# Opening of the prompt attention: constant loads on GpSimd's queue, cache copies behind the fourth store, bias turned after two projections

## The chip, the cores and the metric

The kernel runs on one NeuronCore of a Trainium2 chip. Each engine works through its own list of instructions strictly in order: TensorE (PE, with its weight loads as PEld), VectorE (DVE), ScalarE (ACT), GpSimd (POOL) and SyncE (SP). SP computes nothing; it issues the DMA transfers, and POOL can issue transfers too, on a queue of its own, between its arithmetic. The metric is device time in microseconds (us) for one execution. Two kernels are called different from about 0.2% on.

## The reference

One inference step of a decoder layer, for a prompt of 2048 tokens and 8 single-token samples, width 1024:

```python
q_a, k_a, v_a, q_g, k_g, v_g, r_g, log_a = project(rmsnorm(xp, attn_norm_g), w_in, ...)
o_a = prompt_window_attention(q_a, k_a, v_a, rel_bias, attn_sinks)   # 128-row blocks, own and previous keys
o_g, s_p = gla_chunked(q_g, k_g, v_g, log_a, s0)                     # gated linear attention
xp = finish(xp, o_a, o_g, r_g, ...)                                  # W_o, residual, SwiGLU feed-forward
# the same for the 8 samples, with cached keys and values; their window is shifted by one position:
k_win_sample = concat(cache_k, k_new)[:, -128:]
v_win_sample = concat(cache_v, v_new)[:, -128:]
```

The softmax attention adds a bias that depends only on the distance of query and key (a table `rel_bias` of 32 buckets by 8 heads) and has one learned sink per head. Queries and keys are normalised per head, with gains `q_norm_g` and `k_norm_g`.

## The kernel before, in words

The program has three stages: A, the projections for the softmax attention and the attention itself, in 16 blocks of 128 tokens; B, the gated linear attention; C, the output projection and the feed-forward part by one level of Strassen products. Every float32 product is made of three matmuls on a high and a low part (`mm3`, L107 to L109): high by high, high by low, low by high. `split` (L95 on ACT, L96 on DVE) makes the two parts, so each weight that comes in is cast by ACT and subtracted by DVE before PE may use it.

The part at stake is the first 60 us of stage A. `front(b)` (L290 on) loads a block `xt` of the input, squares and sums it on ACT (L134), forms the variance on DVE (L114, `rs_v`), takes the power -1/2 on POOL (L115, `rs_r`), scales the block on DVE (L137), transposes it in eight matmuls on PE (L142, tile `ps_nT`) and splits it into `nT`. The first block's tile is `xt_181` in the lists below. `load_wq`, `load_wkv`, `load_lr` fill `WA`, the 784 columns of the weights for queries, keys, values and the gate's low rank; `load_wr` fills `WR`, 512 columns. `project(b)` multiplies a block with `WA` (24 matmuls of 512 columns and 24 of 272), `project_r(b)` with `WR` (24 of 512), `attend(b)` does the attention and ends with a store of its output to `mix_d` in DRAM (L422). `load_gains` (L209) loads the gains and sinks, `make_bias` (L521) builds the bias: it loads `rb`, `oh`, `aq`, `afterK` and `flip`, multiplies `rb` with `oh` (L536, `ps_ext`), stores the 8 x 256 result in DRAM (`ext_d`), reads it back with overlapping rows (`rev`, L546) and turns it with the matrix `flip` on PE (L548, `ps_rev`). `decode_a` is the samples' attention, advanced a piece per block.

What sets the order: the code is written once, and when the program is built a scheduler lays out each engine's list by its own estimate of when each instruction's inputs will be there. So a line that moves in the code, or goes to another queue, can shift instructions of other lines. A second rule concerns transfers: SP's issues use eight counters in turn (`DMAHW0` to `DMAHW7` in the lists, `DMASW0` to `DMASW7` for POOL's), and an issue that comes round to a counter waits until the transfer that used it before has landed.

Of the kernel before, what the change touches and what calls it, by code (L numbers as in the profile page):

```python
# [20 lines left out]
P = 128  # L21
# [5 lines left out]
HD = 64  # L27
# [19 lines left out]
def bcast_rows(ap_1d, n, parts=P):  # L47
    return bass.AP(ap_1d.tensor, ap_1d.offset, [[0, parts], [1, n]])
# [3 lines left out]
def hymba_kernel(ctx: ExitStack, tc: tile.TileContext, I, O, X=None, phases=3):  # L52
    nc = tc.nc
# [12 lines left out]
    mix_d = [dram.tile([P, KD, P], F32, name=f"mix_d{i}") for i in range(NB)]  # L66
# [27 lines left out]
    def split(h, l, src, eng=None):  # L94
        nc.scalar.copy(h, src)  # L95
        (eng or nc.vector).tensor_tensor(l, src, h.bitcast(F32), ALU.subtract)  # L96
# [50 lines left out]
    with ExitStack() as ph:  # L147
# [58 lines left out]
        gkB = pc.tile([P, HD], F32, name="gkB")  # L206
        sinkB = pc.tile([P, 8], F32, name="sinkB")

        def load_gains():  # L209
            for g, nm in ((gq, "q_norm_g"), (gk, "k_norm_g")):  # L210
                for h in range(2):
                    nc.sync.dma_start(g[h * 64:(h + 1) * 64], I[nm].rearrange("o d -> d o"))
            nc.vector.tensor_scalar(gq, gq, 0.125, None, ALU.mult)
            nc.sync.dma_start(sinkB, bcast_rows(I["attn_sinks"], 8))
            nc.sync.dma_start(gkB, bcast_rows(I["k_norm_g"], HD))

# [3 lines left out]
        afterK = pc.tile([P, P], F32, name="afterK")  # L222
# [11 lines left out]
        def dense(nT, n, W, c0, c1):  # L234
            ps = acc.tile([P, 512], F32, tag="acc", name="ps_d")
            for k in range(KD):
                mm3(ps[:n, :c1 - c0], nT[:, 0, k, :n], nT[:, 1, k, :n], W[:, 0, k, c0:c1], W[:, 1, k, c0:c1],
                    k == 0, k == KD - 1)
            return ps
# [11 lines left out]
        def gate_r(ps, n):  # L251

            r = rp.tile([P, 512], F32, tag="r", name="r", bufs=2)
            t = rp.tile([P, 512], F32, tag="rt", name="rt", bufs=1)
            nc.scalar.copy(r[:n], ps[:n])
            nc.gpsimd.tensor_scalar(t[:n], r[:n], -87.0, None, ALU.max)
            nc.scalar.activation(t[:n], t[:n], AF.Exp, scale=-1.0)
            nc.scalar.activation(t[:n], t[:n], AF.Ln, bias=1.0)
            nc.scalar.activation(t[:n], t[:n], AF.Exp, scale=-1.0)
            nc.gpsimd.tensor_tensor(r[:n], r[:n], t[:n], ALU.mult)  # L260
            return r
# [92 lines left out]
        def project_r(b):  # L354
            pr = dense(nTs.pop(b), P, WR, 0, 512)
            r = gate_r(pr, P)
            nc.sync.dma_start(r_d[b], r)

        def attend(b):
# [4 lines left out]
            nm = small.tile([P, 8], F32, tag="nm", name="nm")  # L364
# [3 lines left out]
            for v in range(2):  # L368
                St = sp.tile([P, 4, P], F32, tag="S", name="S")
                S.append(St)  # L370
                for c2 in range(2):
                    ps = scp.tile([P, 512], F32, tag="sc", name="ps_s")
                    for c in (2 * c2, 2 * c2 + 1):
                        o = (c % 2) * 256
# [7 lines left out]
                    for c in (2 * c2, 2 * c2 + 1):  # L382
                        o = (c % 2) * 256
                        h = 4 * v + c
# [5 lines left out]
                for c in range(4):  # L390
                    h = 4 * v + c
# [6 lines left out]
            o = wl.tile([P, 512], F32, tag="o", name="o", bufs=2)  # L398
            ol = wl.tile([P, 512], F32, tag="ol", name="ol", bufs=1)
            lo, hi = slice(0, 64), slice(64, 128)  # L400
            for v, (rh, rl) in enumerate(((lo, hi), (hi, lo))):
# [17 lines left out]
                        nc.tensor.matmul(po, dv[:, v], pa[:, i], start=False, stop=i == 1)  # L419
                nc.scalar.copy(ol[rh], po[rl])  # L420
                nc.vector.tensor_tensor(o[rh], po[rh], ol[rh], ALU.add)
            nc.sync.dma_start(mix_d[b][:, 0:4, :], o.rearrange("p (c t) -> p c t", c=4))  # L422

        def decode_a():
            with ExitStack() as decs:
# [95 lines left out]
        def make_bias():  # L521


            with tc.tile_pool(name="a_ext", bufs=1) as ep:
                rb = ep.tile([N_BUCKETS, 8], F32, name="rb")
                nc.sync.dma_start(rb, I["rel_bias"])
                oh = ep.tile([N_BUCKETS, 256], F32, name="oh")
                nc.sync.dma_start(oh, I["c_onehot"])
                aq = ep.tile([P, P], F32, name="aq")
                nc.sync.dma_start(aq, I["c_after"][0])  # L530
                nc.vector.tensor_copy(afterQ, aq)
                nc.sync.dma_start(afterK, I["c_after"][1])
                flip = ep.tile([P, P], F32, name="flip")
                nc.sync.dma_start(flip, I["c_flip"])
                ps = aux.tile([P, 512], F32, tag="aux", name="ps_ext")
                nc.tensor.matmul(ps[:8, :256], rb, oh, start=True, stop=True)  # L536
                ext = rp.tile([P, 512], F32, tag="rt", name="ext", bufs=1)[:8, :256]
                nc.scalar.copy(ext, ps[:8, :256])
                nc.sync.dma_start(ext_d, ext)

                nc.sync.dma_start(dbias_d[:, 1:P], ext[:, 0:P - 1])
                nc.sync.dma_start(dbias_d[:, 0:1], ext[:, P - 1:P])

                for g in range(2):
                    rev = ep.tile([P, 4, P], F32, tag="rev", name="rev", bufs=2)
                    nc.sync.dma_start(rev, bass.AP(ext_d.tensor, ext_d.offset + g * 1024, [[1, P], [256, 4], [1, P]]))  # L546
                    ps = ppp.tile([P, 512], F32, tag="pp", name="ps_rev")
                    nc.tensor.matmul(ps, flip, rev.rearrange("p h j -> p (h j)"), start=True, stop=True)  # L548
                    nc.vector.tensor_copy(bias[:, 4 * g:4 * g + 4].rearrange("p h j -> p (h j)"), ps)
# [8 lines left out]
        load_wkv(0)  # L558
        load_wkv(4)
        load_gains()  # L560
        make_bias()
        for k in range(0, KD, 2):
            load_wr(k)
        project(0)
        project(1)
        project_r(0)
        project_r(1)
        dec = decode_a()
        for b in range(NB):
            if b + 2 < NB:  # L570
                front(b + 2)
            if 1 < b + 1 < NB:
                project(b + 1)
                if b + 1 < NB - 2:
                    project_r(b + 1)
            attend(b)
            if b >= 1:
                next(dec, None)
            if b == 3:
                nc.sync.dma_start(gg, I["gla_norm_g"].rearrange("o d -> d o"))  # L580
                w2 = pc.tile([16, 256], F32, name="w2")
                nc.sync.dma_start(w2, I["w_gla_gate2"][0])
                split(w3[0:16], w3[64:80], w2)
                nc.vector.tensor_copy(w3[32:48], w3[0:16].bitcast(F32))
                for p in range(2):
                    nc.sync.dma_start(bT[:, p:p + 1], I["b_gla_gate"][0:1, p * P:(p + 1) * P].rearrange("o d -> d o"))
                nc.gpsimd.tensor_scalar(nbT, bT, -1.0, None, ALU.mult)
                for nm_, cache in (("k_win_sample", "cache_k"), ("v_win_sample", "cache_v")):
                    nc.sync.dma_start(O[nm_][0, :, 0:P - 1].rearrange("n t h d -> n t (h d)"),
                                      I[cache][0, :, 1:P].rearrange("n t h d -> n t (h d)"))  # L590
        project_r(NB - 2)
        project_r(NB - 1)
    if phases < 2:
# [890 lines left out]
```

## Time and profile before

| | us |
|---|---|
| median of 3 runs (2256.2 to 2256.39) | 2256.27 |
| the profiled execution | 2255.43 |
| its span, first to last instruction | 2253.3 |
| PE busy in it | 2186.8 (97%) |
| DVE, ACT, POOL busy | 1584.1, 981.7, 687.1 |
| clock granted to TensorE, mean | 0.991 |

The profiled execution is 0.84 us below the median, and 2.1 us of it lie outside the span. The views used below are: the list of who waited for whom; the timeline of one engine (start, duration, what, and in brackets the idle time before it with what ended it); tables of busy time by stretches of the span, with the granted clock and the DMA engines' share; groups of instructions by line; and the list of transfers with their sizes. A matmul's duration in the timeline overlaps that of the next one, so the cost of one in a row of them is read from the distance of two starts.

### The profile page before, as it was taken

Reading aid. Unit: us, or ns where it says so; the run is one execution under the profiler, and the core shown is the slowest. Engines: PE = TensorE matmul, PEld = TensorE weight load, DVE = VectorE, ACT = ScalarE, POOL = GpSimd, SP = SyncE. Lnnn points to the kernel's source line nnn. Section 1 sums busy time; section 2 is a strip of 40 time slices with the busy share of each in tenths; the row PEclk is TensorE's granted clock in tenths of the full one; section 3 lists DMA queues with packets and bytes.
Section 4 is the critical chain, followed back from the end, with each engine's and each line's share of the span. In section 5 each row is a group of like instructions: output and inputs, shape, how many; then the busy total and the mean of one; then the engine's idle time right before and its main releaser. Section 6 shows DMA issues by size and latency. Waiting matters only on the chain.

```text
span 2253.3 us, 34780 instructions
## 1 busy us (share of the span) xinstructions
PE 2186.8 (97%) x12573; PEld 1886.2 (84%) x12573; DVE 1584.1 (70%) x3129; ACT 981.7 (44%) x2249; POOL 687.1 (30%) x781
## 2 busy tenths in 40 slices
PE   7999998999998999999999999999999899999997
PEld 5788887888886888688888889999999878787886
DVE  6788888777865666766666666676766765757487
ACT  5656666465654334333333333333333344434342
POOL 2555665564653223211111120111111122222222
PEclk9999999999999999999999999999999999999999
DMA  7323325444507998942333385333333477879786
GB/s 226 110 76 119 118 77 188 133 156 157 184 24 268 318 326 263 327 127 81 112 97 111 95 284 183 90 104 89 113 97 92 152 189 178 195 169 234 165 210 232
DMA packets 212331, 364.32 MB, mean 162 GB/s; under 512 B 15768, under 2 KB 129456, under 8 KB 209072
## 3 DMA queue, kind: packets, MB, share of 16 engines
q1 hardware_dynamic: 175104, 258.63, 35.2%
q0 software_dynamic: 37056, 103.47, 18.1%
q8 instruction: 99, 1.62, 0.3%
q14 instruction: 72, 0.59, 0.1%
HBM read 210.83 MB, written 152.29 MB: 161 GB/s over the span
## 4 chain that ended last, share of the span: by engine, by line
PE 74%; DVE 10%; issue 6%; DMA 5%; ACT 4%; POOL 2%; SPq 0%; POOLq 0%; DVEq 0%; ACTq 0%
PE ps_b L108 7%; PE ps_b L107 7%; PE ps_b L109 7%; PE ps_c L108 5%; PE ps_c L107 5%; PE ps_c L109 5%; PE ps_a L108 5%; PE ps_a L107 5%; PE ps_a L109 5%; PE ps_wo L107 3%; PE ps_wo L108 3%; PE ps_wo L109 3%; DMA z<-zc_d_P 1%; PE ps_l L850 1%; PE ps_v L107 1%
## 5 line engine op out<-in xcount | busy, mean ns | idle before, releaser
L107 PE MATMUL ps_b<-z,whl 128*128 128x258 f32 (+1 forms) x792 | 254.1, 321 | 1.2 <-ACT whl L95 1.2
L109 PE MATMUL ps_b<-z,whl 128*128 128x258 f32 (+1 forms) x792 | 253.0, 319 | 1.6 <-DVE whl L96 1.6
L108 PE MATMUL ps_b<-z,whl 128*128 128x258 f32 (+1 forms) x792 | 254.3, 321 | 0.0
L95 ACT CAST dm<-mr 128x384 fp32r<-128x384 f32 (+1 forms) x224 | 108.5, 488 | 188.3 <-PE ps_b L109 105.2
L108 PE MATMUL ps_a<-z,whl 128*128 128x258 f32 (+1 forms) x528 | 169.2, 320 | 0.0
L108 PE MATMUL ps_c<-z,whl 128*128 128x258 f32 (+1 forms) x528 | 169.1, 320 | 0.0
L109 PE MATMUL ps_a<-z,whl 128*128 128x258 f32 (+1 forms) x528 | 168.9, 320 | 0.0
L107 PE MATMUL ps_c<-z,whl 128*128 128x258 f32 (+1 forms) x528 | 168.7, 319 | 0.3 <-DMA z<-zc_d_P 0.3
L109 PE MATMUL ps_c<-z,whl 128*128 128x258 f32 (+1 forms) x528 | 168.9, 320 | 0.0
L107 PE MATMUL ps_a<-z,whl 128*128 128x258 f32 (+1 forms) x528 | 168.8, 320 | 0.0
L109 PEld LDWEIGHTS ps_b<-z,whl 128*128 128x128 f32 x792 | 149.4, 189 | 14.4 <-DVE whl L96 2.3
L107 PEld LDWEIGHTS ps_b<-z,whl 128*128 128x128 f32 x792 | 149.5, 189 | 13.1 <-ACT whl L95 1.3
L108 PEld LDWEIGHTS ps_b<-z,whl 128*128 128x128 f32 x792 | 149.4, 189 | 11.9
L96 DVE TENSOR_TENSOR dm<-mr,dm 128x384 fp32r<-128x384 f32 (+1 forms) x224 | 115.1, 518 | 57.4 <-ACT dm L95 57.3
L95 ACT CAST whl<-wrg 128x512 fp32r<-128x512 f32 x132 | 81.5, 619 | 154.8 <-PE ps_b L109 81.3
L1316 POOL DMA_DIRECT2D md_d<-m x22 | 15.7, 712 | 360.7 <-DVE m L1279 360.7
L1017 DVE TENSOR_TENSOR gu<-ps_c,gu 128x512 f32<-128x512 f32 (+1 forms) x130 | 77.9, 599 | 59.5 <-PE ps_c L109 58.8
L96 DVE TENSOR_TENSOR whl<-wrg,whl 128x512 fp32r<-128x512 f32 x132 | 90.7, 688 | 37.9 <-ACT whl L95 37.5
L845 POOL TENSOR_TENSOR bd<-E,qTb 64x256 f32<-64x256 f32 x112 | 102.2, 913 | 41.4 <-ACT E L833 26.5
L95 ACT CAST whl<-sy 128x512 fp32r<-128x512 f32 x88 | 54.6, 620 | 132.1 <-PE ps_b L109 84.7
L107 PEld LDWEIGHTS ps_c<-z,whl 128*128 128x128 f32 x528 | 99.8, 189 | 8.6 <-issue 0.7
L107 PEld LDWEIGHTS ps_a<-z,whl 128*128 128x128 f32 x528 | 99.7, 189 | 8.0
(404 smaller groups left out, 6683.6 us busy)
## 6 DMA issues: line engine op xcount, KB each, us to landing
mr<-md_d SPq DMA_DIRECT2D x24, 1344.0 KB
zc_d_P<-zhl POOLq DMA_DIRECT2D x56, 512.0 KB, 6.5
z<-zc_d_P SPq DMA_DIRECT2D x14, 2048.0 KB
wrg<-in_w_gate_dram SPq DMA_DIRECT2D x44, 512.0 KB
wrg<-in_w_up_dram SPq DMA_DIRECT2D x44, 512.0 KB
nT_d<-nT SPq DMA_DIRECT2D x16, 1024.0 KB
zT<-nT_d SPq DMA_DIRECT2D x8, 2048.0 KB
h_d<-gu POOLq DMA_DIRECT2D x48, 256.0 KB, 4.7
```

The source lines that it names most:

```text
L95: nc.scalar.copy(h, src)
L96: (eng or nc.vector).tensor_tensor(l, src, h.bitcast(F32), ALU.subtract)
L107: nc.tensor.matmul(ps, lh, rh, start=start, stop=False, skip_group_check=more)
L108: nc.tensor.matmul(ps, lh, rl, start=False, stop=False, skip_group_check=more)
L109: nc.tensor.matmul(ps, ll, rh, start=False, stop=stop, skip_group_check=more)
L845: nc.gpsimd.tensor_tensor(bv[rows, h], E5[rows, :, :, 1], qv[rows, :, :, 1], ALU.mult)
L850: nc.tensor.matmul(ps[:, g * P:(g + 1) * P], Ef[:, g * P:(g + 1) * P], bd[:, :, g], start=True, stop=True)
L1017: nc.vector.tensor_tensor(out, a, b, ALU.add)
L1316: nc.gpsimd.dma_start(md_d[sb][g][:, :, q, fp - GROUPS[g][0], :], src.rearrange("p (m t) -> p m t", m=4))
```

## The change

Three edits, none of which changes what is computed:

- the eleven small loads of `load_gains` and of `make_bias` (gains, sinks, the bias table, masks, the flip matrix; the largest have 64 KB) are issued by POOL in place of SP;
- `make_bias` becomes a generator with one stop: up to the stores of the 8 x 256 table it runs where it stood, its second part (`rev`, the turning matmul, the copy to `bias`) comes in the code after `project(0)` and `project(1)`;
- the two DRAM-to-DRAM copies of the cached keys and values into the samples' windows (508 KB each) may be issued only after the store of the fourth block's attention output.

```diff
         def load_gains():
             for g, nm in ((gq, "q_norm_g"), (gk, "k_norm_g")):
                 for h in range(2):
-                    nc.sync.dma_start(g[h * 64:(h + 1) * 64], I[nm].rearrange("o d -> d o"))
+                    nc.gpsimd.dma_start(g[h * 64:(h + 1) * 64], I[nm].rearrange("o d -> d o"))
             nc.vector.tensor_scalar(gq, gq, 0.125, None, ALU.mult)
-            nc.sync.dma_start(sinkB, bcast_rows(I["attn_sinks"], 8))
-            nc.sync.dma_start(gkB, bcast_rows(I["k_norm_g"], HD))
+            nc.gpsimd.dma_start(sinkB, bcast_rows(I["attn_sinks"], 8))
+            nc.gpsimd.dma_start(gkB, bcast_rows(I["k_norm_g"], HD))
...
-            nc.sync.dma_start(mix_d[b][:, 0:4, :], o.rearrange("p (c t) -> p c t", c=4))
+            return nc.sync.dma_start(mix_d[b][:, 0:4, :], o.rearrange("p (c t) -> p c t", c=4))
...
-                nc.sync.dma_start(rb, I["rel_bias"])
+                nc.gpsimd.dma_start(rb, I["rel_bias"])
...
-                nc.sync.dma_start(flip, I["c_flip"])
+                nc.gpsimd.dma_start(flip, I["c_flip"])
...
                 nc.sync.dma_start(dbias_d[:, 0:1], ext[:, P - 1:P])
+                yield
...
-        make_bias()
+        turn = make_bias()
+        next(turn)
         for k in range(0, KD, 2):
             load_wr(k)
         project(0)
         project(1)
+        next(turn, None)
...
-            attend(b)
+            stored = attend(b)
...
-                for nm_, cache in (("k_win_sample", "cache_k"), ("v_win_sample", "cache_v")):
-                    nc.sync.dma_start(O[nm_][0, :, 0:P - 1].rearrange("n t h d -> n t (h d)"),
+                with tc.issue_after(stored.ins):
+                    for nm_, cache in (("k_win_sample", "cache_k"), ("v_win_sample", "cache_v")):
+                        nc.sync.dma_start(O[nm_][0, :, 0:P - 1].rearrange("n t h d -> n t (h d)"),
```

How the lists move. DVE, at the start of the program, before; `xt_181` is the first input block, `xt` the second, `WA` the weights of the first projection:

```order
L114 TENSOR_SCALAR rs_v<-ss 128x1 [waits Activation_49]
L137 SCALAR_TENSOR_TENSOR xt_181<-xt_181,rs_r,gB 128x1024 [waits DMAHW1_49,DMAHW0_49,Pool_49]
L96 TENSOR_TENSOR WA<-wr,WA 128x512 [waits DMAHW2_49,Activation_49]
L96 TENSOR_TENSOR WA<-wr,WA 128x512 [waits DMAHW3_49,Activation_49]
L96 TENSOR_TENSOR WA<-wr,WA 128x512 [waits DMAHW4_49,Activation_49]
L96 TENSOR_TENSOR nT<-ps_nT,nT 128x512 [waits Activation_49]
```

DVE at the same place in the changed program, from the row after the first `rs_v` to the first `nT`:

```order
L96 TENSOR_TENSOR WA<-wr,WA 128x512 [waits DMAHW0_49,Activation_49]
L114 TENSOR_SCALAR rs_v<-ss 128x1 [waits Activation_49]
L137 SCALAR_TENSOR_TENSOR xt_181<-xt_181,rs_r,gB 128x1024 [waits DMAHW1_49,Pool_49]
L137 SCALAR_TENSOR_TENSOR xt<-xt,rs_r,gB 128x1024 [waits DMAHW1_49,Pool_49]
L96 TENSOR_TENSOR WA<-wr,WA 128x4x256 [waits DMAHW2_49,Activation_49]
L96 TENSOR_TENSOR WR<-wr,WR 128x1024 [waits DMAHW3_49,Activation_49]
L96 TENSOR_TENSOR w_130<-w_1699,w_130 16x256 [waits DMAHW5_49,Activation_49]
L587 CAST w_130<-w_130 16x256
L96 TENSOR_TENSOR WA<-wr,WA 128x8x16 [waits DMAHW6_49,Activation_49]
L96 TENSOR_TENSOR nT<-ps_nT,nT 128x512 [waits Activation_49]
```

The scaling of the first block now stands behind the second block's `rs_v`, and ahead of the first `nT` stand two scalings, three weight pieces and the gate's small weight `w_130`. PE's list in the changed program, from its first row:

```order
L142 MATMUL ps_nT<-ident,xt_181 128x128 [waits DVE_49]
L142 MATMUL ps_nT<-ident,xt_181 128x128 x7
L107 MATMUL ps_d<-WA,nT 128x512 [waits Activation_49]
L108 MATMUL ps_d<-WA,nT 128x512
L107 MATMUL ps_d<-WA,nT 128x272 [waits Activation_49]
L536 MATMUL ps_ext<-oh,rb 8x256 [waits DMASW7_49,DMASW6_49]
L142 MATMUL ps_nT<-ident,xt 128x128 [waits DVE_49]
L142 MATMUL ps_nT<-ident,xt 128x128 x3
L109 MATMUL ps_d<-WA,nT 128x512
```

Before, the eight transposes were followed by the 24 wide matmuls of `project(0)`; now, after two wide ones and one narrow one, PE transposes the second block, whose `ps_nT` takes the buffer (there are two) that the first block's first half frees. POOL's list in the changed program, behind the making of `ident`:

```order
L212 DMA gq<-in_q_norm_g_dram 64x1 x2
L212 DMA gk<-in_k_norm_g_dram 64x1 x2
L214 DMA sinkB<-in_attn_sinks_dram 128x8
L215 DMA gkB<-in_k_norm_g_dram 128x64
L526 DMA rb<-in_rel_bias_dram 32x8
L528 DMA oh<-in_c_onehot_dram 32x256
L530 DMA aq<-in_c_after_dram 128x128 [waits DMASW0_49]
L532 DMA afterK<-in_c_after_dram 128x128 [waits DMASW1_49]
L534 DMA flip<-in_c_flip_dram 128x128 [waits DMASW2_49]
L115 TENSOR_TENSOR rs_r<-rs_v,nhalf 128x1 [waits DVE_49] x2
```

Before, the two `rs_r` followed `ident` directly. SP's list loses eleven rows; the two copies of the caches, which stood ahead of `ext_d`, now stand behind the store of `mix_d_76`, and the loads of `WR` move up to where the small loads were.

More of the change, by code (lines that the diff above doesn't have):

```diff
@@ L525, in make_bias @@
                 rb = ep.tile([N_BUCKETS, 8], F32, name="rb")
-                nc.sync.dma_start(rb, I["rel_bias"])
+                nc.gpsimd.dma_start(rb, I["rel_bias"])
                 oh = ep.tile([N_BUCKETS, 256], F32, name="oh")
-                nc.sync.dma_start(oh, I["c_onehot"])
+                nc.gpsimd.dma_start(oh, I["c_onehot"])
                 aq = ep.tile([P, P], F32, name="aq")
-                nc.sync.dma_start(aq, I["c_after"][0])
+                nc.gpsimd.dma_start(aq, I["c_after"][0])
                 nc.vector.tensor_copy(afterQ, aq)
-                nc.sync.dma_start(afterK, I["c_after"][1])
+                nc.gpsimd.dma_start(afterK, I["c_after"][1])
                 flip = ep.tile([P, P], F32, name="flip")
-                nc.sync.dma_start(flip, I["c_flip"])
+                nc.gpsimd.dma_start(flip, I["c_flip"])
                 ps = aux.tile([P, 512], F32, tag="aux", name="ps_ext")
@@ L587, in hymba_kernel @@
                 nc.gpsimd.tensor_scalar(nbT, bT, -1.0, None, ALU.mult)
-                for nm_, cache in (("k_win_sample", "cache_k"), ("v_win_sample", "cache_v")):
-                    nc.sync.dma_start(O[nm_][0, :, 0:P - 1].rearrange("n t h d -> n t (h d)"),
-                                      I[cache][0, :, 1:P].rearrange("n t h d -> n t (h d)"))
+                with tc.issue_after(stored.ins):
+                    for nm_, cache in (("k_win_sample", "cache_k"), ("v_win_sample", "cache_v")):
+                        nc.sync.dma_start(O[nm_][0, :, 0:P - 1].rearrange("n t h d -> n t (h d)"),
+                                          I[cache][0, :, 1:P].rearrange("n t h d -> n t (h d)"))
         project_r(NB - 2)
```

## The prediction

> **What bounds the kernel now.** I read the page's chain first, then who PE waited for, then the busy time by stretches, then the timelines of the first 50 us.
>
> ```profile
> PE 74%; DVE 10%; issue 6%; DMA 5%; ACT 4%; POOL 2%; SPq 0%; POOLq 0%; DVEq 0%; ACTq 0%
> ...
> PE ps_nT L142 <- DVE xt L137: 8.6, 2, 8.0
> PE ps_rev L548 <- DMA rev<-ext_d: 3.5, 1, 3.5
> PE ps_d L107 <- ACT qs L305: 0.7, 1, 0.7
> ```
>
> The chain is PE's for three quarters. Two of PE's longest waits lie in the opening: 8.0 us until the first block is scaled, 3.5 us for the bias to come back from DRAM. A small one, 0.7 us, is for a PSUM tile.
>
> ```profile
> core 0: us, PE busy (x) PEld busy (x) DVE busy (x) ACT busy (x) POOL busy (x), PEclk, DMA share, GB/s
> 8.02:22.00 13.98, 12.66 (x59) 10.09 (x60) 12.62 (x19) 9.78 (x17) 2.10 (x2) 1.00 0.96 286
> 91.40:103.50 12.10, 9.82 (x44) 6.41 (x43) 11.10 (x40) 8.85 (x31) 5.57 (x5) 0.72 0.31 104
> 60.00:720.00 660.00, 635.70 (x3992) 549.56 (x3991) 512.16 (x1241) 410.67 (x1137) 388.82 (x382) 0.99 0.40 130
> ```
>
> From 8 to 22 us PE works 12.66 of 13.98 us while the DMA engines are full (0.96). From 60 to 720 us PE idles 24.3 us of 660. So what PE loses at the start is lost, unless one of those holes swallows it. The changed lists differ from the old ones until the end of stage B (to about 720 us); behind that each engine but SP and POOL has the same order, so I cost nothing there: the work is covered as before.
>
> **The first start of PE.** This is the largest term, and it comes from the lists, not from the loads themselves.
>
> ```profile
> 6.68 1.28 DVE L137 SCALAR_TENSOR_TENSOR xt<-xt,rs_r,gB 128x1024 f32<-128x1024 f32 x1 [1.16 <-DMA gB<-in_attn_norm_g_dram]
> ...
> 14.51 0.15 DVE L114 TENSOR_SCALAR rs_v<-ss 128x1 f32<-128x1 f32 x1 [0.29 <-ACT nT L134]
> ...
> 13.33 1.06 ACT L134 ACTIVATE nT<-xt 128x1024 fp32r<-128x1024 f32 x1 [0.52 <-DMA xt<-in_x_prompt_dram]
> ...
> 8.02 1.97 PE L142 MATMUL ps_nT<-ident,xt 128*128 128x128 f32 x8 [8.02 <-DVE xt L137]
> ```
>
> Before, DVE scales the first block at 6.68 and PE starts at 8.02. In the changed list that scaling stands behind the second block's `rs_v`, which needs the second block: it lands at 13.33 and its `rs_v` ends at 14.66. Hence the first scaling ends at 14.66 + 1.28 = 15.94, and PE starts at 16.0. POOL's loads may push this out: they are now in flight beside the weights.
>
> ```profile
> aq<-in_c_after_dram SPq DMA_DIRECT2D x1, 64.0 KB
> afterK<-in_c_after_dram SPq DMA_DIRECT2D x1, 64.0 KB
> flip<-in_c_flip_dram SPq DMA_DIRECT2D x1, 64.0 KB
> ...
> hdec_d<-h POOLq DMA_DIRECT2D x1, 32.0 KB, 5.2
> ```
>
> The first three are 192 KB, with the eight smaller loads an estimated 256 KB; at the 286 GB/s of the full stretch they take 0.9 us from the second block's load. The last row, a 32 KB transfer of POOL's that landed in 5.2 us, is used further down. PE starts between 16.0 and 16.9.
>
> **When PE really runs.** After eight transposes PE has three matmuls and `ps_ext`, then it waits for DVE's first `nT`, the reader that frees the buffer of the second block's transposes. Ahead of that `nT`, from the end of `rs_v`, DVE has two scalings (2 x 1.28), the 4x256 piece of `WA` and the 1024-wide piece of `WR`, the gate weight and its cast, and an 8x16 piece.
>
> ```profile
> 32.49 1.23 DVE L96 TENSOR_TENSOR WR<-wr,WR 128x1024 fp32r<-128x1024 f32 x1 [0.72 <-ACT WR L95]
> ...
> 37.19 0.41 DVE L96 TENSOR_TENSOR w<-w,w 16x256 fp32r<-16x256 f32 x1
> ...
> 20.37 0.68 DVE L96 TENSOR_TENSOR nT<-ps_nT,nT 128x512 fp32r<-128x512 f32 x1
> ```
>
> Sum: 2.56 + 2 x 1.23 + 0.41 + 0.68 = 6.1, and an estimated 0.5 for the gate weight's cast and the small piece, 6.6 in all. From 14.66 that gives 21.3, with the 0.9 above 22.2. I take 21.8. ACT's half of the same pieces, with the load of `WR` behind 4.5 MB by the list of transfers (17 to 18 us at 286 GB/s), ends within the same time, so it adds nothing.
>
> What had PE done by 22.0 before?
>
> ```profile
> L107 PE MATMUL ps_d<-WA,nT 128*128 128x512 f32 (+1 forms) x15 | 6.1, 405 | 0.2 <-ACT nT L95 0.2
> L108 PE MATMUL ps_d<-WA,nT 128*128 128x512 f32 (+1 forms) x15 | 5.8, 383 | 0.6 <-DVE WA L96 0.6
> L109 PE MATMUL ps_d<-WA,nT 128*128 128x512 f32 (+1 forms) x13 | 4.8, 371 | 0.0
> L142 PE MATMUL ps_nT<-ident,xt 128*128 128x128 f32 x16 | 3.0, 352 | 8.6 <-DVE xt L137 8.6
> ...
> 22.00 0.29 PE L109 MATMUL ps_d<-WA,nT 128*128 128x272 f32 x1
> 22.13 0.29 PE L107 MATMUL ps_d<-WA,nT 128*128 128x272 f32 x1
> ...
> 23.35 0.40 PE L108 MATMUL ps_d<-WA,nT 128*128 128x512 f32 x1
> 23.58 0.39 PE L109 MATMUL ps_d<-WA,nT 128*128 128x512 f32 x1
> ```
>
> 43 products, of which 26 wide and 17 narrow by the timeline, and 16 transposes. The change then has 2, 1 and 8. By distances of starts (0.23 wide, 0.125 narrow, 0.11 a transpose) the missing work is 24 x 0.23 + 16 x 0.125 + 8 x 0.11 = 8.4 us. `ps_ext`, some 0.5 us of PE, is already done. So PE stands 7.9 us behind at 22.0, or **7.7 us** with the restart at 21.8; bounds 7.2 and 8.1.
>
> **What the change gives back.** All weights of both projections are split early, so the 0.7 us for `qs` should go. The bias goes to DRAM some 16 us earlier, since the copies of the caches no longer stand ahead of it:
>
> ```profile
> 33.37 5.38 SPq L589 DMA_DIRECT2D out_v_win_sample_dram<-in_cache_v_dram  x1
> ...
> 47.90 1.10 PE L548 MATMUL ps_rev<-rev,flip 128*128 128x512 f32 x2 [3.46 <-DMA rev<-ext_d]
> 48.43 0.80 PE L109 MATMUL ps_d<-WR,nT 128*128 128x512 f32 x1
> 49.07 0.40 PE L107 MATMUL ps_d<-WR,nT 128*128 128x512 f32 x1
> ...
> 49.77 0.22 PE L376 MATMUL ps_s<-kT,qT 128*128 128x128 f32 x1
> ```
>
> That wait of 3.46 goes at most wholly, and with it 0.4 us in which the matmul at 48.43 took 0.64 to the next start in place of 0.23. But `rev` now stands in PE's list right behind `project(0)`, which PE ends near 22 + 5.1 + 2.9 + 0.9 + 0.9 = 31.8 (22 wide, 23 narrow, 8 transposes, the clock below), while `ext_d` lands behind some 7.3 MB of loads (27 us) and `rev` behind the 1 MB store of `nT` (3.7 us more), near 33. I take a new wait of 1.2, with bounds 0 and 3. The store of `nT` and the loads of `WR` are hidden by PE's 20 us of projections.
>
> **The clock.** PE's first matmuls are slow:
>
> ```profile
> 11.31 0.63 PE L107 MATMUL ps_d<-WA,nT 128*128 128x512 f32 x1
> 11.74 0.52 PE L108 MATMUL ps_d<-WA,nT 128*128 128x512 f32 x1
> 12.10 0.39 PE L109 MATMUL ps_d<-WA,nT 128*128 128x512 f32 x1
> ```
>
> Starts lie 0.43 apart until 3.7 us after PE began, then 0.23. That costs both kernels 1.9 us once. The change works a little at 16.5, stops for 3 us and restarts: if it is slow again for 3.7 us it pays up to 1.7 more, if not 0. I take 0.9. The Trainium skill, "TensorE: Matmul & The Clock Gate", Part 1, says the array runs at half clock until a window of about 3.4 us was busy and falls back after an idle one; the trace's 3.7 us agrees, and by that rule the dearer end, 1.7, is the nearer one.
>
> **POOL's issues.** A transfer that POOL issues takes its time:
>
> ```profile
> L1080 POOL DMA_DIRECT2D hdec_d<-h x1 | 0.6, 557 | 4.9 <-DVE h L620 4.9
> L1129 POOL DMA_DIRECT2D zc_d_P<-zhl x56 | 48.4, 887 | 82.2 <-DVE zhl L96 66.8 <-DVE rs_v L114 14.9 <-DVE zd L1102 0.4
> ...
> 1.84 0.29 POOL masks.py:199 TENSOR_SCALAR_AFFINE_SELECT ident<-ident 128x128 f32<-128x128 f32 x1
> 5.60 0.57 POOL L115 TENSOR_TENSOR rs_r<-rs_v,nhalf 128x1 f32<-128x1 f32 x1 [3.47 <-DVE rs_v L114]
> ```
>
> Eleven at 0.56 to 0.89 are 6 to 10 us from 2.1, so `rs_r` ends between 9 and 12.5, earlier than the 14.7 at which DVE wants it: no cost. What is queued behind these issues is only `rs_r`. DVE's `gq`, ninth in its list, needs POOL's first two loads at about 10.6, seven us after their issue; the one small POOL transfer quoted above took 5.2, so I cost that at nothing too, with 2 us as a bound if they queue behind the weights. SP's eleven issues go, which covers nothing that PE waited for.
>
> The Trainium skill, "DMA: Bandwidth & Descriptors", Issuing engine by pattern, speaks against this edit: simple loads belong on SP's queue, and a POOL transfer's first byte comes about 0.4 us later. By it the sum rises by nothing, for those 0.4 us lie inside the seven; no row here shows the two side by side.
>
> **The copies** need SP's queue for some 5 us in either place; behind the fourth store the next loads of `xt` stand behind them, two blocks ahead of use. Cost 0, and up to 5 where that lead fails.
>
> **Sum.** 7.7 − 0.7 − 3.5 − 0.4 + 1.2 + 0.9 = **+5.2 us** by the first `ps_s`, bounds 2.6 and 8.2. From 60 to 720 us the lists are mixed anew against 24.3 us of idle time; I know of no sign there and allow 4 either way. Against the profiled execution that is 2255.43 + 5.2 = 2260.6; the median lies 0.84 higher, 2261.5. I say **2261**.
>
> **Rivals.** *POOL is slow*: eleven issues at 1.6 us in place of 0.9 would end `rs_r` at 2.1 + 17.6 + 0.6 = 20.3, and the first scaling, due at 14.7, would slip 5.6: 2267. It decides from 1.1 us each on. No row has an issue that long, but none is of 4-byte elements either. Chance 0.12. *The delay is swallowed*: where DVE, not PE, sets the pace, as in 91.4 to 103.5 (DVE 11.10 of 12.10 us, PE at a clock of 0.72), a late PE loses nothing. That stretch holds 2.3 us of idle PE and about 3 us of slow clock; if the opening's low end and 2.6 us of it meet, the time is unchanged, 2256. Chance 0.18. *Faster*: the same stretch is lost because DVE does scalings and splits beside attention; with the bias and `WR` ready by 28 us it could keep up and the whole 5.3 us would go, beside the low end of +2.6 and another 2.5 of the idle time to 720: 2256.3 + 2.6 − 7.8 = 2251. It needs DVE's list there to be shorter, and it has the same instructions. Chance 0.11. *The copies collide* at the fourth block, +5 more, 2266: chance 0.04. *The change does not do what it says*: the lists show it does.
>
> **Chances.** My own case has 0.55, about 2257 to 2265. Changes under 0.2%, 4.5 us, can't be told from none; that bound, 2260.8, runs through my case, so I give its slower side 0.33 and the other 0.22. With the rivals: slower 0.33 + 0.12 + 0.04 = 0.49, the same 0.22 + 0.18 = 0.40, faster 0.11. The range of 8 in 10 is 2253 to 2267, which takes in the swallowed delay and slow POOL.
>
> **What would show it.** PE's first row at 16 to 17 us, not 8; its steady run from about 22; a `rev` wait under 3 us; the first `ps_s` near 55. If PE starts near 8 the reading of DVE's list is wrong; if it starts past 18 POOL is slow; if the first `ps_s` is late and the end is not, a later stage swallowed it.

## The result, and the profile after

| | before | after |
|---|---|---|
| median, us (lowest to highest, runs) | 2256.33 (2256.2 to 2256.91, 4) | 2270.95 (2269.31 to 2272.45, 4) |
| ratio, 95% interval | | 1.006 (1.0049 to 1.0072) |
| the profiled execution, us | 2255.43 | 2271.39 |
| its span, us | 2253.3 | 2269.3 |
| mean granted clock | 0.991 | 0.988 |

The change makes the kernel 14.6 us slower; between the two profiled spans it is 16.0. The prediction was 2261 with a range of 2253 to 2267, so the sign was right and the size far too small.

The opening first. In the changed kernel, VectorE's timeline (start, duration, what, and in brackets the idle time before it with what ended it) from the first `rs_v` to the first `nT`:

```profile
5.67 0.15 DVE L114 TENSOR_SCALAR rs_v<-ss 128x1 f32<-128x1 f32 x1 [4.74 <-ACT nT L134]
...
17.35 0.15 DVE L114 TENSOR_SCALAR rs_v<-ss 128x1 f32<-128x1 f32 x1 [1.03 <-ACT nT L134]
17.45 1.28 DVE L137 SCALAR_TENSOR_TENSOR xt<-xt,rs_r,gB 128x1024 f32<-128x1024 f32 x1
19.18 1.28 DVE L137 SCALAR_TENSOR_TENSOR xt<-xt,rs_r,gB 128x1024 f32<-128x1024 f32 x1 [0.45 <-POOL rs_r L115]
...
23.70 0.68 DVE L96 TENSOR_TENSOR nT<-ps_nT,nT 128x512 fp32r<-128x512 f32 x1
```

The first block's scaling does stand behind the second block's `rs_v`. Between the two `rs_v` VectorE also splits seven pieces of `WA` and scales `gq` (8.05 to 16.33); the list shown with the change leaves out all of these rows but one. ScalarE's timeline says why that `rs_v` comes at 17.35 and not at 14.7: the second block lands late.

```profile
11.46 0.62 ACT L95 CAST WA<-wr 128x512 fp32r<-128x512 f32 x1 [1.86 <-DMA wr<-in_w_in_dram]
...
16.17 1.06 ACT L134 ACTIVATE nT<-xt 128x1024 fp32r<-128x1024 f32 x1 [0.61 <-DMA xt<-in_x_prompt_dram]
```

Before, that square began at 13.33. TensorE's timeline shows the start, the stop and the restart:

```profile
18.79 1.97 PE L142 MATMUL ps_nT<-ident,xt 128*128 128x128 f32 x8 [18.79 <-DVE xt L137]
...
24.44 1.11 PE L142 MATMUL ps_nT<-ident,xt 128*128 128x128 f32 x4 [0.71 <-DVE nT L96]
25.21 0.78 PE L109 MATMUL ps_d<-WA,nT 128*128 128x512 f32 x1
25.78 0.63 PE L107 MATMUL ps_d<-WA,nT 128*128 128x512 f32 x1
26.21 0.63 PE L108 MATMUL ps_d<-WA,nT 128*128 128x512 f32 x1
...
28.34 0.58 PE L107 MATMUL ps_d<-WA,nT 128*128 128x512 f32 x1
28.76 0.39 PE L108 MATMUL ps_d<-WA,nT 128*128 128x512 f32 x1
28.99 0.40 PE L109 MATMUL ps_d<-WA,nT 128*128 128x512 f32 x1
```

After the restart, starts lie 0.43 apart until 28.8, then 0.23. The first product of scores, `ps_s`, comes at 58.2 in place of 49.8.

From there on, the busy time by stretches, cut at the same four places of the program in both kernels: the first `ps_s`, the first `ps_dd` (the samples' projection), the first `ps_g` (stage B) and the first `ps_zT` (stage C). The columns are from:to, length, then busy time and instructions of PE, PEld, DVE, ACT and POOL, the granted clock, the DMA engines' share and GB/s. Before:

```profile
49.70:97.70 48.00, 45.02 (x258) 38.23 (x258) 37.35 (x122) 31.09 (x91) 25.52 (x28) 0.96 0.34 104
97.70:389.80 292.10, 284.35 (x1663) 243.05 (x1661) 251.12 (x750) 195.01 (x584) 175.69 (x181) 0.99 0.37 117
389.80:730.90 341.10, 324.53 (x2163) 282.62 (x2162) 238.42 (x414) 194.37 (x487) 192.79 (x181) 0.99 0.45 151
```

After:

```profile
58.20:107.70 49.50, 44.29 (x257) 38.12 (x255) 39.83 (x136) 32.06 (x100) 24.79 (x28) 0.96 0.29 89
107.70:403.30 295.60, 286.26 (x1663) 245.09 (x1662) 254.45 (x733) 193.66 (x574) 181.18 (x182) 0.98 0.38 119
403.30:751.90 348.60, 327.49 (x2164) 285.43 (x2163) 228.36 (x411) 193.99 (x484) 190.92 (x180) 0.98 0.44 146
```

The same matmuls take 1.5, 3.5 and 7.5 us longer, 12.6 with unrounded ends. PE idles 3.0, 7.8 and 16.6 us before, 5.2, 9.3 and 21.1 after, which is 8.4 of it; the rest is PE's busy time, at a granted clock of 0.98 in place of 0.99. The idle part belongs to the lists, as the experiments show; the busy part varies from one execution to the next by as much. In the last stretch the waits have changed places. PE's waits (who waited <- for whom: us, times, longest), after:

```profile
PE ps_l L855 <- POOL bd L850: 6.8, 9, 1.9
PE ps_l L855 <- DVE E L851: 3.7, 2, 3.0
PE po L904 <- DVE dg L875: 3.3, 1, 3.3
```

Before, the wait for `bd` was 1.1 us in all, and the longest ones were others:

```profile
PE ps_m L934 <- ACT r L930: 5.2, 1, 5.2
PE po L899 <- DVE AT L860: 4.1, 4, 1.2
...
PE ps_l L850 <- POOL bd L845: 1.1, 1, 1.1
```

Stage C takes 1513.3 us before and 1512.3 after, counted from the first `ps_zT` to POOL's last issue of the output. And the end is shorter. The queue's own instructions on the last line of the program, before (durations in ns: shortest, median, longest):

```profile
L1480 POOLq DRAIN  x3: 40/102/8357, 2244.1 to 2253.0; - x3
```

After:

```profile
L1485 POOLq DRAIN  x3: 46/98/4352, 2264.1 to 2269.0; - x3
```

POOL's last long DRAIN follows its last issue and sets the end of the program: 8.36 us before, 4.35 after. The stores' data don't explain its length: by the trace's records of single DMA packets, the last one of POOL's queue ended at 2246.1 before and at 2266.1 after, 6.4 and 2.9 us ahead of the DRAIN's end. So the 16.0 us are +8.4 in the opening, +12.6 from there to stage C, -1.0 in stage C and -4.0 at the end.

### The profile page after: what moved, and what is told of

Read it like the earlier page. It is cut to its first block, busy times and chain, and to the rows that moved or that the text cites. A ratio compares the mean times of both kernels' runs of the same rounds, so it can differ in the third digit from the quotient of the medians.

```text
span 2269.3 us, 34782 instructions
## 1 busy us (share of the span) xinstructions
PE 2192.3 (97%) x12573; PEld 1892.0 (83%) x12573; DVE 1579.7 (70%) x3129; ACT 982.2 (43%) x2249; POOL 697.5 (31%) x792
## 4 chain that ended last, share of the span: by engine, by line
PE 73%; DVE 9%; issue 7%; POOL 4%; DMA 3%; ACT 3%; SPq 0%; POOLq 0%; DVEq 0%
PE ps_b L108 7%; PE ps_b L107 7%; PE ps_b L109 7%; PE ps_a L108 5%; PE ps_c L108 5%; PE ps_c L107 5%; PE ps_a L109 5%; PE ps_c L109 5%; PE ps_a L107 5%; PE ps_wo L107 3%; PE ps_wo L109 2%; PE ps_wo L108 2%; PE ps_d L108 2%; PE ps_d L107 2%; PE ps_d L109 2%
```

## The experiments

The columns: the ratio to the kernel before (95% interval); from each profiled execution, the start of the first `ps_s`, the time from there to the first `ps_zT`, the time from POOL's last issue of the output to the end of the span, and the span. "Kept" means that PE's list is that of before, or differs from it in at most 153 lines; "new" means thousands of lines. Each row from a profile is one execution: with the old lists alone, the first `ps_s` comes at 47.3 to 49.8 and the way to stage C takes 680.6 to 684.8, so differences of up to 2.5 and 4.2 us in these two columns say nothing.

| kernel | PE's list | ratio | first `ps_s` | to stage C | last issue to end | span |
|---|---|---|---|---|---|---|
| before | | 1 | 49.8 | 681.1 | 9.1 | 2253.3 |
| after | new | 1.006 (1.0049 to 1.0072) | 58.2 | 693.7 | 5.1 | 2269.3 |
| e1_loads | new | 1.0076 (1.0059 to 1.0092) | 57.1 | 692.0 | 5.1 | 2266.3 |
| e2_copies | new | 1.0049 (1.0034 to 1.0064) | 45.4 | 695.2 | 9.1 | 2262.6 |
| e4_copies_turn | new | 1.0028 (1.0016 to 1.004) | 45.6 | 692.7 | 9.1 | 2260.3 |
| e5_late | new | 1.0045 (1.0028 to 1.0061) | 52.9 | 697.3 | 5.1 | 2267.5 |
| e6_fifth | new | 1.0078 (1.0058 to 1.0098) | 58.2 | 694.1 | 5.1 | 2270.1 |
| e7_rb | new | 1.0048 (1.0033 to 1.0063) | 51.6 | 692.5 | 9.1 | 2265.9 |
| e8_tiny | new | 1.0044 (1.0029 to 1.0059) | 50.3 | 692.3 | 9.1 | 2265.2 |
| e10_gains | new | one run, 2271.81 us | 48.6 | 698.1 | 9.1 | 2269.7 |
| e11_rows | kept | 1.000 (0.9991 to 1.0009) | 47.8 | 683.4 | 9.1 | 2254.8 |
| e9_ystore | kept | 0.9974 (0.9965 to 0.9984) | 47.3 | 684.8 | | 2249.0 |
| e12_split | kept | 0.9977 (0.9967 to 0.9986) | 49.2 | 680.6 | 4.0 | 2246.9 |
| e13_ystore8 | kept | 0.997 (0.9958 to 0.9981) | 49.4 | 682.6 | | 2249.4 |

One edit isn't in the table: turning the bias later, alone, leaves every row of every engine's list as it was, so there was nothing to run. The later turn only matters beside another edit.

### One edit at a time

Only the eleven loads on POOL (e1_loads):

```diff
-                    nc.sync.dma_start(g[h * 64:(h + 1) * 64], I[nm].rearrange("o d -> d o"))
+                    nc.gpsimd.dma_start(g[h * 64:(h + 1) * 64], I[nm].rearrange("o d -> d o"))
...
-                nc.sync.dma_start(flip, I["c_flip"])
+                nc.gpsimd.dma_start(flip, I["c_flip"])
```

> Only the eleven small loads go to POOL's queue; the copies of the caches and the bias stay as in the kernel before. All lists are then those of the changed kernel from the second block on, and the opening's lists too but for a few rows. Theory 1 (the opening and the later lists each cost their own part: the first score matmul ps_s came 8.4 us later, the start of stage C 21.1 us later): PE starts near 18.8, first ps_s near 58, stage C 20 to 22 us later than before, time 2268 to 2273. Rival (the copies behind the fourth store cost the later part): first ps_s near 58, stage C only about 8 us later, time 2256.3 + 8.4 = 2265 or less.

Only the copies tied to the fourth store (e2_copies):

```diff
-            attend(b)
+            stored = attend(b)
...
-                for nm_, cache in (("k_win_sample", "cache_k"), ("v_win_sample", "cache_v")):
+                with tc.issue_after(stored.ins):
+                    for nm_, cache in (("k_win_sample", "cache_k"), ("v_win_sample", "cache_v")):
```

> Only the copies are tied to the fourth store; the small loads stay on SP. DVE's list has the first scaling early again, while from about the third block to the end of stage B all lists are row for row those of the changed kernel. Theory 1: PE starts at 8.0, first ps_s within 2 us of 49.8, and stage C starts still 11 to 13 us later than before; time about 2267 to 2269. Rival (the later loss is a consequence of the late start): stage C within 2 us of before, time 2255 to 2258. The end of the program, which was 4 us shorter in the changed kernel, shows by its POOL drain whether POOL's eleven transfers did that: as long as before (8.4 us) if they did.

The changed kernel with POOL's loads held until the first block's `rs_r` is done (e5_late; `powers` is the list of the results of L115):

```diff
-                    nc.gpsimd.dma_start(g[h * 64:(h + 1) * 64], I[nm].rearrange("o d -> d o"))
+                    with tc.issue_after(powers[0].ins):
+                        nc.gpsimd.dma_start(g[h * 64:(h + 1) * 64], I[nm].rearrange("o d -> d o"))
...
```

> The changed kernel with POOL's eleven loads put behind the first block's power on POOL. DVE's list has the first scaling early again; the later lists are those of the changed kernel. Theory 1: PE starts near 8, first ps_s at 48 to 52 (the loads still run beside the weights), stage C starts 11 to 13 us later than before, time 2256.3 + 12 less up to 4 at the end, 2263 to 2268. Rival (POOL's loads themselves slow the weights so much that the opening stays lost): first ps_s at 55 or later, time 2268 or more.

The copies and the turn of the bias as changed, the loads left on SP (e4_copies_turn):

```diff
+                yield
...
-        make_bias()
+        turn = make_bias()
+        next(turn)
...
+        next(turn, None)
...
+                with tc.issue_after(stored.ins):
```

> Copies behind the fourth store and the bias turned later, small loads on SP. The opening's lists are nearly those of the kernel before; the later lists differ from both kernels'. Theory 1 makes the later lists a cost of their own that need not be the changed kernel's: PE starts at 8.0, first ps_s at 46 to 51 (the wait of 3.5 us for the bias gone or not), and stage C anywhere from 3 us earlier to 13 us later; time 2253 to 2270. Rival (the two edits do what they are for and the lists do not matter): stage C 3 to 4 us earlier, time 2252 to 2254.

The loads alone give nearly the whole loss, in the opening (57.1) and behind it (692.0); tying the copies as well adds nothing that can be told from the spread, so the copies do not collide with later loads. The copies alone bring the first `ps_s` to 45.4, 1.9 to 4.4 us earlier than the kernels with the old lists, since the bias no longer waits for its way through DRAM: PE's wait for `rev` (3.5 us before, 1.4 to 2.4 in the other four with old lists) is gone in that kernel. Yet it ends 9.3 us later than before. With the loads held back, or with the loads on SP, PE starts at 8.0 as before, and the way to stage C is long all the same. (In e5_late the first `ps_s` is late nevertheless, since PE waits 4.5 us for a piece of `WA`.) Several of the expected numbers were missed: stage C starts 18.2 us later than before in e1_loads, 9.7 in e2_copies and 19.3 in e5_late, where 20 to 22, 11 to 13 and 11 to 13 were expected. Whatever the opening does, the later part costs 11 to 16 us more than before. What these four kernels have in common is that their lists are new.

### Do the lists themselves cost?

The copies at the fifth store in place of the fourth, everything else as changed (e6_fifth):

```diff
+            if b == 4:
+                with tc.issue_after(stored.ins):
+                    for nm_, cache in (("k_win_sample", "cache_k"), ("v_win_sample", "cache_v")):
...
-                with tc.issue_after(stored.ins):
-                    for nm_, cache in (("k_win_sample", "cache_k"), ("v_win_sample", "cache_v")):
```

> All three edits, but the copies are tied to the fifth store in place of the fourth. In its lists DVE's first scaling is back in row 5, and all rows of PE, DVE, ACT and POOL are those of e2_copies apart from the loads and the turned bias. Theory 1 (the place of the scaling costs the opening, the later lists cost about 10 us by themselves, POOL's short last drain gives 4 back): POOL's eleven issues hold rs_r until about 10.1, so PE starts near 12, the first ps_s comes near 49, the first matmul of stage C near 744, the span is 2261 to 2264, with a last drain of 4.35. Theory 2 (the later cost is only the late opening carried on): with the first ps_s where it was before, the first matmul of stage C comes near 731 as before and the span is 2249 to 2251.

This expectation describes lists that the kernel doesn't have. VectorE's first scaling stands in it where it stands in the changed kernel; its trace has it at 17.18, right behind the second `rs_v`. So the run tells neither theory apart. It shows that one block more or less for the copies changes nothing: the first `ps_s` at 58.2 and 694.1 us to stage C, as in the changed kernel.

One load of 1 KB on POOL and nothing else (e7_rb):

```diff
-                nc.sync.dma_start(rb, I["rel_bias"])
+                nc.gpsimd.dma_start(rb, I["rel_bias"])
```

> The kernel before with one load of 1 KB, rb, issued by POOL and nothing else. In its lists the later rows are those of e2_copies. Theory 1 (the lists cost by themselves): PE starts at 8.0, and yet the first matmul of stage C comes at 740 to 745 in place of 730.9, with the POOL wait for bd of about 7 us, span 2262 to 2267 with a last drain of 8.35, 4 less if one more POOL transfer is enough to shorten the drain. Theory 2 (lists do not matter): 2253 to 2254.

And the two loads of repeated rows, 4 KB and 32 KB (e11_rows):

```diff
-            nc.sync.dma_start(sinkB, bcast_rows(I["attn_sinks"], 8))
-            nc.sync.dma_start(gkB, bcast_rows(I["k_norm_g"], HD))
+            nc.gpsimd.dma_start(sinkB, bcast_rows(I["attn_sinks"], 8))
+            nc.gpsimd.dma_start(gkB, bcast_rows(I["k_norm_g"], HD))
```

> The kernel before with the two loads of repeated rows (sinkB, gkB) issued by POOL. Its lists stay nearly those of before: 153 lines of difference on PE, where one load of 1 KB (e7_rb) had thousands. Theory 1 (the later lists cost by themselves): stage C starts at 729 to 733, no POOL wait for bd beyond 1.1 us, ratio 0.998 to 1.001. Theory 2 (POOL's transfers at the start cost, whatever the lists): 4 to 10 us slower as in e7_rb. The square of the second block: 13.3 to 13.6 if the gains of e10_gains hold the weights back, 15 to 16 if these do.

These two decide it. One load of 1 KB makes the kernel 0.48% slower, two loads of 36 KB together make no difference that can be measured. The first one's `ps_s` comes 1.8 us later, which is within the spread, but its way to stage C is 11.4 us longer, and the waits of stage B are those of the changed kernel. The same three stretches of e7_rb:

```profile
51.60:101.30 49.70, 44.07 (x258) 37.85 (x257) 38.24 (x140) 34.05 (x102) 24.98 (x26) 0.95 0.35 106
101.30:397.20 295.90, 286.04 (x1662) 244.51 (x1661) 254.25 (x733) 192.74 (x573) 181.73 (x182) 0.98 0.37 114
397.20:744.10 346.90, 327.25 (x2164) 284.82 (x2162) 227.94 (x411) 194.46 (x485) 190.52 (x180) 0.98 0.44 148
```

PE's waits in its third stretch:

```profile
PE ps_l L850 <- POOL bd L845: 6.7, 9, 1.9
PE ps_l L850 <- DVE E L846: 3.7, 2, 3.0
PE po L899 <- DVE dg L870: 2.8, 1, 2.8
```

The stretches of e11_rows, whose PE list differs from that of before in 153 lines where e7_rb's differs in thousands, and not at all from the first `ps_s` to stage C if operation, tiles and shapes are compared:

```profile
47.80:95.00 47.20, 43.90 (x258) 37.51 (x257) 36.13 (x121) 30.70 (x90) 25.63 (x28) 0.98 0.35 106
95.00:388.90 293.90, 286.01 (x1663) 244.72 (x1662) 251.87 (x753) 195.73 (x585) 175.83 (x182) 0.98 0.38 116
388.90:731.20 342.30, 326.44 (x2164) 284.57 (x2162) 236.79 (x412) 193.25 (x484) 192.13 (x181) 0.98 0.45 150
```

The table says the same for every kernel: 680.6 to 684.8 us to stage C in the five with the old lists, 692.0 to 698.1 in the nine with new ones, and no overlap. PE's idle time on that way separates the two groups further: 27.0 to 28.4 us with the old lists, 33.3 to 39.5 with new ones, while its busy time overlaps (653.4 to 657.4 and 654.8 to 663.1; 658.0 in the changed kernel and 654.8 in e1_loads, whose PE lists are the same there). PE's wait for `bd` is 1.1 us in all five and 5.5 to 6.9 in all nine. Theory 1 stands: the order of the later rows, with the waits it brings, costs by itself. But the nine are not nine draws. From the first `ps_s` to stage C the changed kernel, e1_loads and e6_fifth have the same PE list row for row (by operation, tiles and shapes), and those of e2_copies, e5_late and e7_rb, some 3630 rows each, differ from it in 106 to 131 lines; only e4_copies_turn, e8_tiny and e10_gains have orders of their own. So four other orders came up, and all four were worse. Which pair of rows in them is the costly one, these runs don't tell. I made no experiment that takes away the wait for `bd` alone, since any edit to stage B mixes the lists again.

### What holds back the weights at the start?

The six small loads alone (e8_tiny: both gains in two halves each, `sinkB`, `gkB`), and the four gain loads alone (e10_gains):

```diff
-                    nc.sync.dma_start(g[h * 64:(h + 1) * 64], I[nm].rearrange("o d -> d o"))
+                    nc.gpsimd.dma_start(g[h * 64:(h + 1) * 64], I[nm].rearrange("o d -> d o"))
...
-            nc.sync.dma_start(sinkB, bcast_rows(I["attn_sinks"], 8))
-            nc.sync.dma_start(gkB, bcast_rows(I["k_norm_g"], HD))
+            nc.gpsimd.dma_start(sinkB, bcast_rows(I["attn_sinks"], 8))
+            nc.gpsimd.dma_start(gkB, bcast_rows(I["k_norm_g"], HD))
```

> The kernel before with the six loads of gains and sinks (elements of 4 bytes and rows that are repeated) issued by POOL, the five larger loads of the bias stay with SP; its lists are those of e7_rb but for the loads. If these six loads keep the weights back, the second block's square on ACT starts near 16 in place of 13.3 and the first ps_s is 2 to 3 us behind e7_rb; if the five larger ones did it, it starts at 13.3 to 13.6. The last drain is 4.35 if six POOL transfers shorten it, 8.35 if it takes more.

> The kernel before with the four gain loads (64 rows of one 4-byte element each) issued by POOL. If these hold back the weights, as the six loads of e8_tiny did, the second block's square on ACT starts at 15 to 16; if the two loads of repeated rows did it, at 13.3 to 13.6. Its later lists are new ones, so the first matmul of stage C comes 8 to 14 us after 730.9 by the theory that the lists cost by themselves.

e8_tiny's lists are not e7_rb's, as its expectation has it: VectorE's first scaling stands four rows further back (12.71 us), so its first `ps_s` can't be compared as planned. Nor does the second block's square tell when the block landed in these two kernels (15.74 and 14.49): ScalarE has no idle time before it there. The weights do. ScalarE's fourth cast of `WA` in e8_tiny:

```profile
11.45 0.62 ACT L95 CAST WA<-wr 128x512 fp32r<-128x512 f32 x1 [1.51 <-DMA wr<-in_w_in_dram]
```

In the changed kernel it came at 11.46 after a wait of 1.86, before at 9.71 without a wait. So six loads of 37 KB in all hold this piece back as long as the eleven of 262 KB do. The table by stretches of 2 us, before:

```profile
8.00:10.00 2.00, 1.99 (x9) 1.71 (x9) 1.93 (x4) 1.97 (x4) 0.00 (x0) 1.00 1.05 406
```

e8_tiny:

```profile
8.00:10.00 2.00, 0.00 (x0) 0.00 (x0) 1.41 (x3) 1.31 (x3) 0.00 (x0) 1.00 1.04 217
```

The DMA engines are as full (1.05 and 1.04) and move half the bytes (406 and 217 GB/s). The trace's records of single packets name the load that does it. In these two microseconds, 32 us of the 16 engines' time, the packets of POOL's queue take 13.7 us in e8_tiny, and nearly all of that belongs to `sinkB`: its 4 KB, the same 32 bytes for each of 128 rows, go as 16 packets of 256 bytes that took 0.9 us each (median), 12.9 us in all, while the 16 packets of `gkB` (32 KB) took 1.3 us and the 4-byte packets 9 ns each. In the changed kernel `sinkB` took 14.7 us of engine time, more than the three loads of 64 KB together (8.7). In the kernel before, issued by SP from 15.1 on, the same load goes as 128 packets of 32 bytes and takes 0.9 us of engine time. So what a load costs here follows neither its bytes nor the number of its packets. Why POOL's packets of repeated rows are so slow isn't shown.

The single kinds agree. The gain loads alone leave the traffic as it was (392 GB/s from 8 to 12 us in e10_gains, 405 before). With `sinkB` and `gkB` alone, `sinkB` again takes 12.8 us, from 6.0 on, and the second block's square starts at 14.40 behind a wait of 0.56 for the block, 1.1 later than before; with `rb` alone it starts at 13.32. And where the lists stay (e11_rows) this costs the program nothing that can be measured. The Trainium skill, "DMA: Bandwidth & Descriptors", Why small descriptors are slow, says that each packet carries a fixed overhead of a few cycles; that isn't what was paid here, where the smallest packets took 9 ns and `sinkB`'s 0.9 us.

### The end of the program

Sixteen of the output's 32 stores cut into halves, so POOL issues 16 transfers more (e12_split):

```diff
-                        nc.gpsimd.dma_start(O["y_prompt"][0, ti * P:(ti + 1) * P, cols], hq[which])
+                        for part in range(2 if 2 <= mi < 6 else 1):
+                            w = 256 if 2 <= mi < 6 else 512
+                            here = slice(part * w, (part + 1) * w)
+                            nc.gpsimd.dma_start(O["y_prompt"][0, ti * P:(ti + 1) * P, cols][:, here], hq[which][:, here])
```

> The kernel before with sixteen of the output's 32 stores cut into two halves, so POOL issues 16 more transfers of the same bytes; PE's list is as before but for 10 lines. If the number of POOL transfers decides the length of its last drain (8.35 us with none, one or six more, 4.35 with eleven more), the drain is 4.35 and the span about 2249 to 2250; if the early place or the kind of the eleven loads does, it is 8.35 and the span 2253 to 2254.

The last four stores on SP (e9_ystore), and the last eight (e13_ystore8, with `mi >= 6`):

```diff
-                        nc.gpsimd.dma_start(O["y_prompt"][0, ti * P:(ti + 1) * P, cols], hq[which])
+                        (nc.sync if mi == 7 else nc.gpsimd).dma_start(O["y_prompt"][0, ti * P:(ti + 1) * P, cols], hq[which])
```

> The kernel before, with the last four stores of the output issued by SP in place of POOL; all other rows are as before. If POOL's last drain of 8.35 us starts after POOL's own last issue and only it sets the end, POOL is through by about 2247 and the span is 2247 to 2249. If the drain waits for every transfer in flight, or SP's own end takes as long, the span stays at 2252 to 2254.

> The kernel before with the last eight stores of the output issued by SP. In e9_ystore (four) POOL's drain of 8.35 us still set the end, 2.5 us behind SP's last issue. If POOL's drain follows its own last issue, it is through some 4 us earlier and the end is set by the last store's landing, at 2247 to 2248.5: 1 to 2 us below e9_ystore. If a store of SP's queue now holds a load behind it, the end is 1 to 4 us above e9_ystore.

The queue's own instructions on the last line, of e12_split and then of e9_ystore and e13_ystore8:

```profile
L1483 POOLq DRAIN  x3: 46/93/3231, 2242.9 to 2246.6; - x3
```

```profile
L1480 POOLq DRAIN  x3: 46/93/8027, 2240.0 to 2248.8; - x3
```

```profile
L1480 POOLq DRAIN  x3: 40/102/7703, 2232.9 to 2249.1; - x3
```

With 16 POOL transfers more, at another place and of another kind than the eleven loads, the last DRAIN takes 3.23 us: so neither the early place nor the kind of those loads made it shorter. In e9_ystore POOL's last issue ends 4.2 us earlier, at 2240.5, and the DRAIN of 8.03 is over at 2248.5. In e13_ystore8 it is over at 2241.1, long before the end: there the last of SP's stores sets it, whose last packet ended at 2247.8. SP's timeline of e13_ystore8, and of e9_ystore:

```profile
2235.82 10.69 SPq L1407 DMA_DIRECT2D out_y_prompt_dram<-hq  x7
```

```profile
2240.31 6.15 SPq L1407 DMA_DIRECT2D out_y_prompt_dram<-hq  x4
```

Both issue their last store by 2246.5, and both end near 2249: in e9_ystore the two ends were already level, where the last expectation took POOL for the later one. That is why moving eight stores gains no more than moving four. All three versions beat both kernels: 2249.64, 2250.81 and 2249.02 us against 2256.02 to 2256.3 of the kernel before beside them.

## Why the prediction was wrong

**The first start of PE: right in its cause, 1.9 to 2.8 us short.** The scaling behind the second `rs_v` was the reason, as the prediction read from the lists. The term that failed is the estimate for POOL's 256 KB, 0.9 us by bytes: the second block came 2.84 us later. Ahead of it POOL's packets took 29 us of engine time, 1.8 us if spread over 16 engines (an estimate from the packet records), and half of that was the 4 KB of `sinkB`; how the rest of the 2.84 comes about stays open.

**The restart.** 21.8 was predicted, 24.44 came; of these 2.6 us, 2.3 are the same late block (2.84 less the 0.5 that lay in the 21.8).

**The clock: the dearer end.** 0.9 was taken, 1.7 was paid: seven starts 0.43 apart in place of 0.23, and the 0.57 at 25.21. PE worked from 18.79, but with holes; none of its starts was fast before the restart at 24.44, and they stayed slow until 28.8. By the rule of the Trainium skill ("TensorE: Matmul & The Clock Gate", Part 1), the array runs at half clock until a window of about 3.4 us was busy. The trace agrees, with 4.3 us from the restart to the first fast start.

**The bias.** The 0.7 for `qs` is gone and the wait for `rev` too, as predicted. The new wait of 1.2 didn't come: `ps_rev` ran at 35.35 and 45.55 without idle time: `rev` was issued at 27.4 and 28.6, and PE came to it late. The 0.4 behind a `ps_rev` stayed. That the whole 3.5 of `rev` could be given back was in part luck of the execution read: the other four with old lists waited 1.4 to 2.4 there.

**Sum of the opening.** 5.2 + 2.6 (restart) + 0.8 (clock) - 1.2 (`rev`) + 0.4 = 7.8 of the measured 8.4, just outside the bounds of 2.6 to 8.2. A term for the other 0.6 is missing from the prediction: the second `ps_rev`, at 51.36 behind the first `ps_s` before, now stands ahead of it at 45.55 and takes some 0.9 us there. With executions that spread over 2.5 us in the opening, the sum can't be tested more finely than that.

**"I know of no sign there and allow 4 either way": the step that failed most.** The lists mixed anew cost 12.6 us from the first `ps_s` to stage C, of which 8.4 are new idle time of PE; its wait for `bd` alone grew by 5.7. It had a sign: all nine kernels with new lists lose 10.9 to 17.0 us there against the old one, whatever edit made them new. The prediction gave the old order no advantage over the new one; the runs show it to be better than the four others that came up.

**Behind stage B "I cost nothing there".** Right for stage C (-1.0), wrong for the end: the drain became 4.0 us shorter, as in all four kernels in which POOL issues eleven transfers more. This shortening kept the miss from being larger still, which is luck. No row of a single profile told that; the 8.36 us could be seen in it, and that they set the end.

**The rivals.** *POOL is slow* is out, although the prediction named a start of PE past 18 as its sign, and PE started at 18.79: its issues took 0.50 to 0.61 us each, `rs_r` was ready at 10.75, long before 17.45, though its ninth issue waited for the first transfer:

```profile
8.39 0.57 POOL L530 DMA_DIRECT2D aq<-in_c_after_dram  x1 [1.95 <-DMA gq<-in_q_norm_g_dram]
...
10.05 0.70 POOL L115 TENSOR_TENSOR rs_r<-rs_v,nhalf 128x1 f32<-128x1 f32 x1
```

*The delay is swallowed* and *faster* are out, since the delay grew. *The copies collide* is out by e1_loads. The rule "Issuing engine by pattern" of the Trainium skill ("DMA: Bandwidth & Descriptors"), that simple loads belong on SP, spoke against the edit. The edit was bad, but no run separates the 0.4 us of a later first byte that the prediction costed beside that rule; what showed in the opening was the engine time of POOL's packets, and with the lists kept (e11_rows) even that of `sinkB` cost nothing that could be measured.

## What to carry to other kernels

Where a scheduler lays out the lists, an edit of one small load can cost more by the rows it moves hundreds of microseconds later than by itself: here 10 us for 1 KB. So compare the whole lists first, treat a reshuffle of a well-running order as a possible loss of its own (here four orders of four lost), and test an edit's own worth in a form that keeps the lists (e11_rows). Price small loads beside saturated engines by what their packets take in a trace, not by their bytes (here 4 KB took more engine time than 192 KB), and look at what the program does after its last store: it was the cheapest gain here.

## What the runs showed of the hardware that was not expected

- POOL's last DRAIN took 8.35 us with the POOL transfers of before and with one, two, four or six more, 4.35 with eleven more, 3.23 with sixteen more, 8.03 with four fewer and 7.70 with eight fewer. It isn't a straight line in that number. Before, POOL's last packet had ended 6.4 us ahead of the DRAIN's end; what it does in the time isn't shown.
- Six loads of 37 KB took the DMA engines from 406 to 217 GB/s for two microseconds while they stayed full, nearly all by the 4 KB of `sinkB`: 16 packets of 0.9 us from POOL's queue, where SP's 128 packets for the same load took 7 ns each.
- The granted clock differs between executions where PE's list doesn't. From 340 to 400 us, before and after:

```profile
340.00:400.00 60.00, 53.94 (x311) 45.12 (x310) 49.25 (x144) 40.66 (x119) 37.40 (x36) 0.97 0.51 167
```

```profile
340.00:400.00 60.00, 54.03 (x311) 46.41 (x311) 52.61 (x156) 40.83 (x125) 35.85 (x33) 0.91 0.52 166
```

The clock is 0.97 and 0.91, but the lists don't decide it: e11_rows, with the old ones, has 0.91 in this stretch, and e1_loads, with the changed kernel's PE list, has 0.97. What lowers it isn't shown.
